# Three gate tiles move from stage 3 of a hybrid RG-LRU and attention layer into its recurrent stage, and work changes engines in the feed-forward stage

## The chip, the cores and the metric

The kernel runs on one core of a Trainium2 chip. The metric is the device time of one execution in microseconds (us); lower is better. The engines are PE (TensorE: matmuls), DVE (VectorE), ACT (ScalarE), POOL (GpSimd) and SP (SyncE, which issues nearly all DMAs). Each of them works through its own queue in order, and semaphores order them against each other.

## The reference: what is computed

Two requests of 512 tokens by 1024 features go through one layer with shared weights. Cut to what matters here:

```python
proj = rmsnorm(x) @ w_in            # 9216 columns, cut into lru_x, lru_gate, q, k, v, gates
xc = dwconv(lru_x)                  # 1280 channels, 4 taps
h = rglru(xc, forward) + rglru(xc, backward)
#   per direction, 16 blocks of 80 channels: r, i = sigmoid(xb @ wa), sigmoid(xb @ wx)
#   a = exp(-8 r softplus(-lam)); u = sqrt(1 - a*a) * i * xc; h[t] = a[t] h[t-1] + u[t]
a_out = (gelu(lru_gate) * h) @ w_lru_out
b_out = dilated_window_attention(q, k, v) @ w_att_out     # 3 groups, merged by their lse
x = x + (sigmoid(g_a) * a_out + sigmoid(g_b) * b_out) @ w_o
gate, val = split(rmsnorm(x) @ w_up)                      # 2 x 3072 columns
x = x + (gelu(dwconv(gate)) * val) @ w_down
```

All is float32.

## The kernel before, in words

**Products.** An fp32 product is made from halves: each operand is cast to a high half (`hi`) and a low half (`lo`, the difference), and three matmuls per 128-row slice sum hi*hi, lo*hi and hi*lo (`mm3`, `prod`). Weights stream through a ring: `Stream` loads raw 128x512 slabs by SP (up to 3 ahead), splits them (`split_to`: the cast to hi on ACT or DVE, the subtraction to lo at line 230 on the engines listed in `lo_eng`, in turn), and holds at most 8 split slabs (`adv`, `take`, `done`). The scheduler keeps the order in which each engine's instructions are written.

**Stage 1 (to 414 us).** `steps1` lists 10 steps "L" (an LRU input tile, convolved by `lru_conv`) and 16 steps "G" (a tile of the attention and LRU gates, through a tanh to DRAM). A step is two halves of 24 matmuls, one for each request. After each half `lru_slot(LRU_RATE)` adds its rate to a credit (capped at 1.5) and, at a credit of 1, issues the next item of recurrent work: `lru_first(n)` (one direction of block n: 8 small matmuls `psg` at lines 456 and 457, tanh and exp on ACT, two DVE products at 467 and 468; then the scan of block n-1) or `lru_second(n)` (the other direction, and the preparation of block n+2). A gate product waits in PSUM until DVE has taken the one before it.

**Stage 2 (to about 974 us).** q, k and v for three groups, with attention between.

**Stage 3 (to about 1096 us).** Ten gate tiles c = 0 to 9 of lru_gate, two halves each, `h_load`, gelu, times h: request 0 stays in SBUF (`held`, `y_split`), request 1 goes to `y_d`. In the first `ATT_DONE` = 3 tiles the attention runs out. Tile c also loads the three attention results of token tile c-2 (`comb_load`, into a ring of six `cg` buffers) and merges them three ticks later (`combine`: DVE, then two adds on POOL at 876 and 877). For token tiles 4 to 7 the merged tile is stored to `o_d` by POOL's queue one tick later. `defer(n, f)` runs f at the n-th next `tick`; there is one tick per half, and the calls due at one tick run in the order in which they were deferred. What is left runs in a loop of ticks at the stage's end.

**Mix and w_o (to about 1352 us).** `th_load` fetches the tanh tiles, into SBUF bytes that the `cg` ring had; `mix_tile` makes 42 matmuls and hands its PSUM tile (two of them) to DVE at 1002 and 1003.

**FFN (to 1865 us).** Each of 24 tiles of w_up is made in a form with 7 products of 12 matmuls in place of 8, which needs sums of weight pieces (`up_split`: S1 = A21 + A22, S2 = S1 - A11, S3 = A11 - A21, S4 = A12 - S2, at line 259, on POOL) and sums of the input (`sums_T`, whose PSUM tile is taken from the pool "t" for the last two token tiles). `batch0(f)` makes the two products A11 and A12; then its PSUM tile `pa` is copied to `p1` by DVE (line 1213; by ACT for f below `EARLY` = 4). `rest(f)` adds the product of S2 into the same `pa`, so that this product waits for the copy; then follow S1, S3, S4 and A22, the convolution on DVE (1246, 1248), the gelu on ACT (1250), and two products on DVE (1252, 1257). After each product `prod` calls `ws.done` and `ws.adv`, and only then does its caller issue the DVE read of the result:

```python
pa, pb = bank(nm), bank("B")
prod(pa, ws.take(1)[0], "B11", True)      # matmuls; then ws.done, ws.adv -> up_split of a later slab
p1[f] = row("p1", 2)
A.copy(out=p1[f], in_=pa) if f < EARLY else V.tensor_copy(out=p1[f], in_=pa)
```

With the ring full, the slab split there is the one eight further on: after A11 of tile f it is A12 of tile f+1, which is the call of `up_split` that makes S1 and S2; S3 and S4 follow the split of S2, one product later.

**Down.** 12 pairs of hidden tiles (`h_pair`: cast on ACT, low halves on the two engines named) times w_down; each PSUM tile `psd`, of eight, is added into the output by DVE at 1330.

Of the kernel before, what the change touches and what calls it, by code (L numbers as in the profile page):

```python
# [20 lines left out]
T = 1024  # L21
# [13 lines left out]
NEG = -1e30  # L35
LRU_RATE = 0.9
O_ORDER = ((0, 0), (0, 1), (1, 0), (1, 1))
# [76 lines left out]
def layer_kernel(ctx: ExitStack, tc: tile.TileContext, xs_in, norm1_g, w_in, conv_w, conv_b, lru_wa, lru_ba,  # L114
# [17 lines left out]
    h_d = dram.tile([RNN, T], F32, name="h_d")  # L132
    y_d = dram.tile([RNN, S], F32, name="y_d")
    sg_d = dram.tile([2 * D, T], F32, name="sg_d")
# [44 lines left out]
    for c in range(3, KR):  # L179
        steps1 += [("G", c - 3), ("L", c)]  # L180
    steps1 += [("G", c) for c in range(KR - 3, 16)]
    specs = []
    for t, c in steps1:
        specs += col_slabs(w_in, C_LRU + 128 * c if t == "L" else C_GA + 128 * c, KD)
    for i in range(9):
        base = (C_V, C_K, C_Q)[i % 3] + 512 * (i // 3)
        specs += [row_slab(w_in, k, base, "ab"[i % 2]) for k in range(KD)]
    for c in range(KR):
        specs += col_slabs(w_in, C_GATE + 128 * c, KD)
# [67 lines left out]
    def up_split(f, nm):  # L257
        w = lambda key: upw[f, key]
        add = lambda out, x, y, op: G.tensor_tensor(out=out, in0=x, in1=y, op=op)
        if nm == ("S2" if f < EARLY else "A12"):  # L260
            upw[f, "S1"] = up_pool[0].tile([128, 512], F32, tag="s1", bufs=1, name="s1")
            upw[f, "S2"] = up_pool[0].tile([128, 512], F32, tag="s2", bufs=1, name="s2")
            add(w("S1"), w("A21"), w("A22"), ALU.add)
            add(w("S2"), w("S1"), w("A11"), ALU.subtract)
        out = split_to("a", w(nm))
        if nm == "S2":
            add(w("A21"), w("A11"), w("A21"), ALU.subtract)
            upw[f, "S3"] = w("A21")
            add(w("A12"), w("A12"), w("S2"), ALU.subtract)
            upw[f, "S4"] = w("A12")  # L270
        if nm == "A22":
            for key in [x for x in upw if x[0] == f]:
                del upw[key]
        return out
# [308 lines left out]
    for s, (typ, c) in enumerate(steps1):  # L583
        if s < 2:
            continue
        slabs = ws.take(2)
        ps = ps1.tile([128, 2, 512], F32, tag="m", bufs=2, name="ps")
        main_mm(ps[:, 0], 0, slabs)
        tick()
        lru_slot(LRU_RATE)  # L590
        main_mm(ps[:, 1], 1, slabs)
        ws.done("a", 2)
        tick()
        ws.adv(2 if s < len(steps1) - 4 else 3)
        if typ == "L":
            lru_conv(c, ps)
        else:
            th = lp.tile([128, 2, S], F32, tag="xc", bufs=2, name="sgt")
            act(out=th, in_=ps, func=AF.Tanh, scale=0.5)
            defer(1, lambda c=c, th=th: SP.dma_start(out=sg_d[128 * c:128 * c + 128],  # L600
                                                     in_=th.rearrange("p b t -> p (b t)")))
        lru_slot(LRU_RATE)
# [301 lines left out]
    ATT_DONE = 3  # L904
    h_load(0)
    for c in range(KR):
        if c == ATT_DONE:
            assert not (units or infl or infl2 or pend)
# [4 lines left out]
            for cc in list(held):  # L913
                y_split(cc, held.pop(cc))
        slabs = ws.take(2)
        for b in range(2):
# [11 lines left out]
            if b == 1:  # L928
                ws.done("a", 2)
                if c + 1 < KR:  # L930
                    h_load(c + 1)
                if c >= 2:
                    cg = comb_load(c - 2)
                    defer(3, lambda t=c - 2, cg=cg: combine(t, cg))
            tick()
            ws.adv(1)
            hT = hts.pop((c, b))
            if b == 0 and c < ATT_DONE:
                gl = p3.tile([128, S], F32, tag="yhold", bufs=ATT_DONE, name="yhold")
# [4 lines left out]
            if b == 1:  # L944
                defer(1, lambda c=c, gl=gl: SP.dma_start(out=y_d[128 * c:128 * c + 128, :], in_=gl))
            elif c < ATT_DONE:
                held[c] = gl
            else:
                y_split(c, gl)
        step[0] += 1  # L950
    lo_eng[:] = [V, G]
    ws.adv(8)
    while later:
# [122 lines left out]
    def hook0(n, i):  # L1076
        if 1 <= n <= KR:
            y_split(n - 1, ystage.pop(n - 1))
        if n < KR:
            ystage[n] = mp.tile([128, S], F32, tag="yst", bufs=3, name="yst")  # L1080
            SP.dma_start(out=ystage[n], in_=y_d[128 * n:128 * n + 128, :])
        if n < 4:
# [199 lines left out]
    banks[1] = batch0(1)  # L1282
    sums(3, pf["t"], "t")
    sums(0)
# [3 lines left out]
    pace[0] = 2  # L1288
    lo_eng[:] = [G]
    sums(1)  # L1290
# [8 lines left out]
    for f in range(NF):  # L1299
# [3 lines left out]
        if f == EARLY:  # L1303
            pace[0] = 2
        pa = banks.get(f) if f < EARLY else batch0(f)
        if f == NF - 1:
            h_pair(0, (V, G))
        rest(f, pa)
    close(cm_f, cm_b, *cm_pf[::-1])


    cm_ps, ps5 = open_pool("ps5", space=PSUM)
    cm_d, dp = open_pool("accd")
    for t in range(8):
        acc[t] = dp.tile([128, D], F32, name=f"accd{t}")
        SP.dma_start(out=acc[t], in_=acc_d[128 * t:128 * t + 128, :])
    for f in range(0, NF, 2):
        w4 = ws.take(4)
        hh, hl = hT.pop(f)
        for t in range(8):  # L1320
            tl = slice(128 * t, 128 * t + 128)
            for hlf in range(2):
                ps = ps5.tile([128, 512], F32, tag="t", bufs=8, name="psd")
                cl = slice(512 * hlf, 512 * hlf + 512)
# [16 lines left out]
        ws.adv(2)  # L1341
    close(cm_d, cm_acc, cm_x20, cm_sa, cm_rp, cm_ps)

# [32 lines left out]
```

## Time and profile before

| | |
|---|---|
| median of 3 runs | 2132.16 us (2132.09 to 2134.18) |
| the profiled execution | 2135.13 us, of which span 2133.4 us |
| mean granted TensorE clock | 0.984 |
| busy: PE, DVE, ACT, POOL | 2032.3, 1259.0, 840.2, 796.0 us |
| moved by DMA | 218.71 MB |

The span runs from the first to the last instruction of the profiled execution; the rest of its time lies around it. Busy times are summed over the span and overlap between engines. A matmul's own duration overlaps the next one's, so the share of PE says little; how many matmuls there are in a stretch says more.

### The profile page before, as it was taken

The page shows a single profiled execution, that of the slowest core. Times are in us where ns is not written, and L with a number is a line of the kernel's source. Part 1 is how long each engine was busy: PE and PEld are TensorE (multiplying, and loading weights), DVE is VectorE, ACT ScalarE, POOL GpSimd, SP SyncE. Part 2 cuts the span into 40 slices and gives each one's busy share as a digit, 9 for nine tenths or more (in the row PEclk, how much of TensorE's full clock was granted, in tenths as well). Part 3 has the DMA queues.
Part 4 walks back from the last instruction along what each step waited for, and adds up shares of the span by engine and source line. Part 5 has one row for each costly group of instructions (what it writes and reads, how often), then busy time and mean ns, then how long its engine had stood idle before and what let it go on. Part 6 is the DMA issues. An engine that isn't in the chain of part 4 may idle for free.

```text
span 2133.4 us, 26437 instructions
## 1 busy us (share of the span) xinstructions
PE 2032.3 (95%) x9571; PEld 1707.6 (80%) x9571; DVE 1259.0 (59%) x1844; ACT 840.2 (39%) x1437; POOL 796.0 (37%) x681
## 2 busy tenths in 40 slices
PE   8989888999999999999999999778899999999999
PEld 6867666787899999998778788657788888788887
DVE  5599998627862671675665565634444444455555
ACT  4488888612431242135433332323333333321210
POOL 3111111034213421413342222487777777632421
PEclk9999999999999999999999999989999999999999
DMA  4535444411111112103556464312222223352322
GB/s 145 155 98 142 122 121 128 157 46 44 31 41 50 35 51 60 30 16 120 193 167 221 160 206 137 105 50 89 89 71 88 81 87 90 124 187 84 107 91 79
DMA packets 203776, 218.71 MB, mean 103 GB/s; under 512 B 28892, under 2 KB 148222, under 8 KB 203646
## 3 DMA queue, kind: packets, MB, share of 16 engines
q1 hardware_dynamic: 201278, 210.73, 31.9%
q0 software_dynamic: 2368, 6.29, 1.1%
q8 instruction: 76, 1.25, 0.3%
q14 instruction: 54, 0.44, 0.1%
HBM read 161.73 MB, written 50.00 MB: 99 GB/s over the span
## 4 chain that ended last, share of the span: by engine, by line
PE 72%; DVE 13%; issue 6%; POOL 4%; ACT 4%; DMA 2%; DVEq 0%; SPq 0%; POOLq 0%; ACTq 0%
PE ps L807 7%; PE ps L808 6%; PE ps L809 6%; PE ps L151 4%; PE ps L153 4%; PE ps L152 4%; PE psd L1328 4%; PE psd L1327 4%; PE psd L1329 4%; PE pfA L1198 3%; PE pfA L1200 3%; PE pfA L1199 3%; DVE u L486 3%; PE o L728 3%; PE pfC L1199 2%
## 5 line engine op out<-in xcount | busy, mean ns | idle before, releaser
L230 POOL TENSOR_TENSOR lo<-raw,hi 128x512 fp32r<-128x512 f32 (+1 forms) x263 | 341.0, 1305 | 640.7 <-ACT hi L227 607.3
L227 ACT CAST hi<-raw 128x512 fp32r<-128x512 f32 (+1 forms) x352 | 204.3, 606 | 302.3 <-PE psd L1329 152.4
L807 PE MATMUL ps<-hi,xh 128*128 128x512 f32 x576 | 251.4, 436 | 0.0
L808 PE MATMUL ps<-lo,xh 128*128 128x512 f32 x576 | 228.4, 397 | 0.0
L809 PE MATMUL ps<-hi,xl 128*128 128x512 f32 x576 | 228.3, 396 | 0.0
L151 PE MATMUL ps<-xh,hi 128*128 128x512 f32 x544 | 216.0, 397 | 0.3 <-DVE xc L403 0.3
L152 PE MATMUL ps<-xl,hi 128*128 128x512 f32 x544 | 214.9, 395 | 0.0
L153 PE MATMUL ps<-xh,lo 128*128 128x512 f32 x544 | 214.1, 394 | 0.0
L1330 DVE TENSOR_TENSOR accd<-accd,psd 128x512 f32<-128x512 f32 x192 | 130.6, 686 | 114.3 <-PE psd L1329 108.9
L807 PEld LDWEIGHTS ps<-hi,xh 128*128 128x128 f32 x576 | 156.1, 271 | 9.6 <-issue 0.2
L808 PEld LDWEIGHTS ps<-lo,xh 128*128 128x128 f32 x576 | 158.3, 275 | 6.0
L809 PEld LDWEIGHTS ps<-hi,xl 128*128 128x128 f32 x576 | 156.3, 271 | 8.0
L1327 PE MATMUL psd<-hi,hp 128*128 128x512 f32 x384 | 150.0, 391 | 3.1 <-DVE gc L1257 3.1
L1329 PE MATMUL psd<-hi,hp 128*128 128x512 f32 x384 | 150.1, 391 | 0.0
L1328 PE MATMUL psd<-lo,hp 128*128 128x512 f32 x384 | 150.1, 391 | 0.0
L707 ACT ACTIVATE p<-p,nm 128x128 f32<-128x128 f32 (+1 forms) x192 | 81.7, 426 | 146.2 <-DVE nm L705 146.1
L1198 PE MATMUL pfA<-T,hi 128*128 128x512 f32 x288 | 116.0, 403 | 23.3 <-DVE p L1213 7.6
L629 DVE TENSOR_REDUCE ss<-sq 128x8 f32<-128x512 f32 x48 | 32.9, 685 | 163.7 <-ACT sq L626 163.7
L151 PEld LDWEIGHTS ps<-xh,hi 128*128 128x128 f32 x544 | 104.2, 192 | 24.5 <-issue 1.4
L153 PEld LDWEIGHTS ps<-xh,lo 128*128 128x128 f32 x544 | 103.8, 191 | 22.2
L152 PEld LDWEIGHTS ps<-xl,hi 128*128 128x128 f32 x544 | 103.9, 191 | 21.8
L1200 PE MATMUL pfA<-T,lo 128*128 128x512 f32 x288 | 114.7, 398 | 1.1 <-POOL lo L230 1.1
(257 smaller groups left out, 4567.3 us busy)
## 6 DMA issues: line engine op xcount, KB each, us to landing
raw<-in_w_in_dram SPq DMA_DIRECT2D x144, 256.0 KB
raw<-in_w_up_dram SPq DMA_DIRECT2D x56, 256.0 KB
r<-in_w_up_dram SPq DMA_DIRECT2D x48, 256.0 KB
f_d<-gc SPq DMA_DIRECT2D x24, 512.0 KB
raw<-in_w_down_dram SPq DMA_DIRECT2D x48, 256.0 KB
hraw<-f_d SPq DMA_DIRECT2D x24, 512.0 KB
sg_d<-sgt SPq DMA_DIRECT2D x16, 512.0 KB
raw<-in_w_lru_out_dram SPq DMA_DIRECT2D x32, 256.0 KB
```

The costliest lines, as they stand in the source:

```text
L151: PE.matmul(out=ps, lhsT=a, rhs=b, start=(k == 0), stop=False)
L152: PE.matmul(out=ps, lhsT=a, rhs=rl(k), start=False, stop=False)
L153: PE.matmul(out=ps, lhsT=wl(k), rhs=b, start=False, stop=(k == n - 1))
L227: A.copy(out=hi[:, 0:n], in_=r[:, 0:n])
L230: e.tensor_tensor(out=lo[:, 0:n], in0=r[:, 0:n], in1=hi[:, 0:n], op=ALU.subtract)
L807: PE.matmul(out=ps, lhsT=a, rhs=hi, start=(k == 0), stop=False)
L808: PE.matmul(out=ps, lhsT=a, rhs=lo, start=False, stop=False)
L809: PE.matmul(out=ps, lhsT=b, rhs=hi, start=False, stop=(k == KD - 1))
L1198: PE.matmul(out=ps, lhsT=a, rhs=bh[:, k], start=(start and k == 0), stop=False, **kw)
L1327: PE.matmul(out=ps, lhsT=hh[:, i, tl], rhs=w[0], start=(i == 0), stop=False)
L1328: PE.matmul(out=ps, lhsT=hh[:, i, tl], rhs=w[1], start=False, stop=False)
L1329: PE.matmul(out=ps, lhsT=hl[:, i, tl], rhs=w[0], start=False, stop=(i == 1))
```

## The change

- `EARLY_Y` = 3: the gate tiles c = 0, 1, 2 become steps "Y" at the end of `steps1`, for both requests at once (gelu, times h loaded from `h_d`, whole rows to `y_d`, which grows to both requests). Stage 3 runs over c = 3 to 9, and loads request 0 of the three early tiles back into the `yhold` buffers. `LRU_RATE` falls from 0.9 to 0.8.
- The merges get a table, `combs`: after tile index i of stage 3 it loads one or two token tiles, and merges them two and three ticks later.
- The four sums of `up_split` go from POOL to DVE. `lo_eng` is [G, V] from before the fourth `batch0` until tile f = 5, and [G] from there (before: [G]). At the end of stage 3 it is [V] for the fill of the ring and [V, G] after it (before: [V, G] for both).
- `sums(3)`, which needs the pool "t", moves behind the third `batch0`. The low halves of the first `h_pair` are both made on POOL.
- The eight PSUM tiles of down come from a pool of six and one of two.

```diff
-LRU_RATE = 0.9
+LRU_RATE = 0.8
+EARLY_Y = 3
-    steps1 += [("G", c) for c in range(KR - 3, 16)]
+    steps1 += [("G", c) for c in range(KR - 3, 16)] + [("Y", c) for c in range(EARLY_Y)]
...
-        add = lambda out, x, y, op: G.tensor_tensor(out=out, in0=x, in1=y, op=op)
+        add = lambda out, x, y, op: V.tensor_tensor(out=out, in0=x, in1=y, op=op)
...
+        elif typ == "Y":
+            gl = lp.tile([128, 2, S], F32, tag="xc", bufs=2, name="gl")
+            ht = lp.tile([128, 2, S], F32, tag="xc", bufs=2, name="ht")
+            SP.dma_start(out=ht.rearrange("p b t -> p (b t)"), in_=h_d[128 * c:128 * c + 128])
+            act(out=gl, in_=ps, func=AF.Gelu_apprx_tanh)
+            V.tensor_tensor(out=gl, in0=ht, in1=gl, op=ALU.mult)
+            defer(1, lambda c=c, gl=gl: SP.dma_start(out=y_d[128 * c:128 * c + 128],
+                                                     in_=gl.rearrange("p b t -> p (b t)")))
...
-    h_load(0)
-    for c in range(KR):
-        if c == ATT_DONE:
+    combs = {2: (0,), 3: (1, 2), 4: (3,), 5: (4, 5), 6: (6, 7)}
+    h_load(EARLY_Y)
+    for c in range(EARLY_Y, KR):
+        i = c - EARLY_Y
+        if i == ATT_DONE:
...
+            for cc in range(EARLY_Y):
+                t = p3.tile([128, S], F32, tag="yhold", bufs=ATT_DONE, name="yback")
+                SP.dma_start(out=t, in_=y_d[128 * cc:128 * cc + 128, 0:S])
+                defer(2, lambda cc=cc, t=t: y_split(cc, t))
...
-                if c >= 2:
-                    cg = comb_load(c - 2)
-                    defer(3, lambda t=c - 2, cg=cg: combine(t, cg))
+                for j, t in enumerate(combs.get(i, ())):
+                    cg = comb_load(t)
+                    defer(2 + j, lambda t=t, cg=cg: combine(t, cg))
...
+    lo_eng[:] = [V]
+    ws.adv(8)
     lo_eng[:] = [V, G]
-    ws.adv(8)
...
-    sums(3, pf["t"], "t")
     sums(0)
     sums(0)
     batch0(2, "C")
     ws.hold = len(specs)
     pace[0] = 2
-    lo_eng[:] = [G]
+    lo_eng[:] = [G, V]
+    sums(3, pf["t"], "t")
...
+        if f == EARLY + 1:
+            lo_eng[:] = [G]
         pa = banks.get(f) if f < EARLY else batch0(f)
         if f == NF - 1:
-            h_pair(0, (V, G))
+            h_pair(0, (G, G))
...
     cm_ps, ps5 = open_pool("ps5", space=PSUM)
+    cm_ps_b, ps5b = open_pool("ps5b", space=PSUM)
+    nd = 0
...
-                ps = ps5.tile([128, 512], F32, tag="t", bufs=8, name="psd")
+                ps = (ps5.tile([128, 512], F32, tag="t", bufs=6, name="psd") if nd % 8 < 6 else
+                      ps5b.tile([128, 512], F32, tag="t", bufs=2, name="psd"))
+                nd += 1
```

## Rows read from the trace of the kernel before

**Rows 1.** The page, part 1: busy us (share of the span) and instructions.

```profile
...
PE 2032.3 (95%) x9571; PEld 1707.6 (80%) x9571; DVE 1259.0 (59%) x1844; ACT 840.2 (39%) x1437; POOL 796.0 (37%) x681
...
```

**Rows 2.** Four stretches: us, busy (count) by engine, clock, DMA share, GB/s.

```profile
...
1352.00:1510.00 158.00, 121.45 (x493) 95.81 (x493) 79.39 (x92) 54.21 (x90) 117.49 (x90) 0.90 0.27 81
1510.00:1853.00 343.00, 343.00 (x1513) 283.59 (x1511) 155.30 (x215) 117.95 (x180) 244.34 (x194) 1.00 0.28 86
974.00:1120.00 146.00, 138.23 (x674) 113.81 (x672) 85.66 (x200) 67.98 (x123) 56.66 (x46) 0.99 0.50 162
81.00:392.00 311.00, 278.19 (x1164) 213.46 (x1163) 283.73 (x280) 261.24 (x258) 35.28 (x42) 0.97 0.44 119
...
```

**Rows 3.** Stage 1: TensorE's longest wait and VectorE's low halves, 100 to 400 us.

```profile
...
PE psg L456 <- DVE u L467: 26.5, 12, 4.4
...
L230 DVE TENSOR_TENSOR lo<-raw,hi 128x512 fp32r<-128x512 f32 x38 | 24.3, 682 | 0.0
...
```

**Rows 4.** Stage 1: the last gate group and the last tanh, timeline.

```profile
...
389.87 0.40 PE L456 MATMUL psg<-x,w 120*80 120x512 f32 x1
...
414.01 1.02 ACT L599 ACTIVATE sgt<-ps 128x1024 f32<-128x1024 f32 x1
...
```

**Rows 5.** Stage 3: one combine, from VectorE's first to GpSimd's last, timeline.

```profile
...
1036.45 0.16 DVE L861 TENSOR_TENSOR cm<-cg 128x8 f32<-128x8 f32 x1
...
1042.13 1.60 POOL L877 TENSOR_TENSOR cg<-cg 128x512 f32<-128x512 f32 x1 [0.68 <-POOL cg L876]
...
1111.17 1.62 POOL L877 TENSOR_TENSOR cg<-cg 128x512 f32<-128x512 f32 x1 [0.69 <-POOL cg L876]
...
```

**Rows 6.** End of stage 3: SP's waits, and TensorE's wait.

```profile
...
SPq L982 <- POOL cg L877: 5.6, 1, 5.6
SPq L853 <- DMA o_d<-cg: 2.6, 2, 2.3
...
1120.83 0.76 PE L151 MATMUL ps<-yh,hi 128*128 128x512 f32 x1 [5.18 <-DVE thb L1003]
...
```

**Rows 7.** FFN start, 1352 to 1510: TensorE's waits (total us, times, longest us).

```profile
...
PE pst L1124 <- ACT T L1143: 11.7, 2, 9.8
PE pfA L1198 <- DVE p L1213: 7.6, 2, 5.6
...
```

**Rows 8.** VectorE and GpSimd on two SBUF inputs each at once, timeline.

```profile
...
1437.51 1.66 DVE L1248 SCALAR_TENSOR_TENSOR gc<-g,vff,gc 128x511 f32<-128x511 f32 x1
...
1439.86 0.75 DVE L1248 SCALAR_TENSOR_TENSOR gc<-g,vff,gc 128x511 f32<-128x511 f32 x1
...
1436.88 1.74 POOL L230 TENSOR_TENSOR lo<-r,hi 128x512 fp32r<-128x512 f32 x1
...
```

**Rows 9.** One steady FFN tile, timeline of VectorE, GpSimd, ScalarE and TensorE.

```profile
...
1617.35 0.68 DVE L1257 TENSOR_TENSOR gc<-gc,pfA 128x512 f32<-128x512 f32 x1
1617.94 0.69 DVE L1213 COPY p<-pfA 128x512 f32<-128x512 f32 x1
...
1617.29 1.30 POOL L230 TENSOR_TENSOR lo<-raw,hi 128x512 fp32r<-128x512 f32 x1 [4.52 <-ACT hi L227]
1618.55 1.29 POOL L259 TENSOR_TENSOR s<-r,r 128x512 f32<-128x512 f32 x1
...
1616.61 1.12 ACT L227 CAST hi<-raw 128x512 fp32r<-128x512 f32 x2
...
1618.96 0.39 PE L1198 MATMUL pfA<-T,hi 128*128 128x512 f32 x1
...
```

**Rows 10.** A wait with no change of pace behind it, TensorE timeline.

```profile
...
1461.30 0.47 PE L1198 MATMUL pfA<-T,hi 128*128 128x512 f32 x1 [3.58 <-DVE u L1230]
...
```

**Rows 11.** End of the FFN and start of down, TensorE and GpSimd timeline.

```profile
...
1855.02 0.47 PE L1198 MATMUL pfA<-T,hi 128*128 128x512 f32 x1 [1.71 <-DVE u L1232]
...
1867.90 0.50 PE L1327 MATMUL psd<-hi,hp 128*128 128x512 f32 x1 [3.08 <-DVE gc L1257]
...
1854.34 2.39 POOL L1275 TENSOR_TENSOR hp<-hraw,hp 128x1024 fp32r<-128x1024 f32 x1 [4.52 <-ACT hp L1274]
...
```

More of the change, by code (lines that the diff above doesn't have):

```diff
@@ L132, in layer_kernel @@
     h_d = dram.tile([RNN, T], F32, name="h_d")
-    y_d = dram.tile([RNN, S], F32, name="y_d")
+    y_d = dram.tile([RNN, T], F32, name="y_d")
     sg_d = dram.tile([2 * D, T], F32, name="sg_d")
@@ L180, in layer_kernel @@
         steps1 += [("G", c - 3), ("L", c)]
-    steps1 += [("G", c) for c in range(KR - 3, 16)]
+    steps1 += [("G", c) for c in range(KR - 3, 16)] + [("Y", c) for c in range(EARLY_Y)]
     specs = []
     for t, c in steps1:
-        specs += col_slabs(w_in, C_LRU + 128 * c if t == "L" else C_GA + 128 * c, KD)
+        specs += col_slabs(w_in, {"L": C_LRU, "G": C_GA, "Y": C_GATE}[t] + 128 * c, KD)
     for i in range(9):
@@ L904, in layer_kernel @@
     ATT_DONE = 3
-    h_load(0)
-    for c in range(KR):
-        if c == ATT_DONE:
+    combs = {2: (0,), 3: (1, 2), 4: (3,), 5: (4, 5), 6: (6, 7)}
+    h_load(EARLY_Y)
+    for c in range(EARLY_Y, KR):
+        i = c - EARLY_Y
+        if i == ATT_DONE:
             assert not (units or infl or infl2 or pend)
@@ L937, in layer_kernel @@
             hT = hts.pop((c, b))
-            if b == 0 and c < ATT_DONE:
+            if b == 0 and i < ATT_DONE:
                 gl = p3.tile([128, S], F32, tag="yhold", bufs=ATT_DONE, name="yhold")
@@ L944, in layer_kernel @@
             if b == 1:
-                defer(1, lambda c=c, gl=gl: SP.dma_start(out=y_d[128 * c:128 * c + 128, :], in_=gl))
-            elif c < ATT_DONE:
+                defer(1, lambda c=c, gl=gl: SP.dma_start(out=y_d[128 * c:128 * c + 128, S:T], in_=gl))
+            elif i < ATT_DONE:
                 held[c] = gl
@@ L1080, in hook0 @@
             ystage[n] = mp.tile([128, S], F32, tag="yst", bufs=3, name="yst")
-            SP.dma_start(out=ystage[n], in_=y_d[128 * n:128 * n + 128, :])
+            SP.dma_start(out=ystage[n], in_=y_d[128 * n:128 * n + 128, S:T])
         if n < 4:
@@ L1341, in layer_kernel @@
         ws.adv(2)
-    close(cm_d, cm_acc, cm_x20, cm_sa, cm_rp, cm_ps)
+    close(cm_d, cm_acc, cm_x20, cm_sa, cm_rp, cm_ps_b, cm_ps)
 _INS = ['x_prompt', 'x_sample', 'norm1_g', 'w_in', 'lru_conv_w', 'lru_conv_b', 'lru_wa', 'lru_ba', 'lru_wx', 'lru_bx',
```

## The prediction

> **What bounds the kernel now.** I read the page's busy shares first: PE 95% [rows 1]. The stretches come second, and there one counts matmuls. In the steady FFN, 1513 matmuls fill 343.00 us: 0.2267 us each at full pace, the unit of all sums below [rows 2]. Stage 1 has 1164 in 311 us. They need 263.9 us, so 47 us are lost, while DVE is busy for 283.7 of the 311: DVE sets that pace, and PE's longest wait there is for DVE's product at line 467 [rows 2, 3]. The start of the FFN has 493 in 158 us, 32 of them short transposes (some 3.5 us); 461 need 104.5 us, so 50 us are lost, POOL is busy for 117.5, and PE waits for results that stand behind POOL's [rows 2, 7]. Stage 3 and the steady FFN are PE's own. The waits come third, and the timeline last, for one question: which DVE instruction has how much time to spare in the steady FFN.
>
> **The three gate tiles, -15 us.** Taken from stage 3: 3 x 48 matmuls, 32.6 us. Given to stage 1: after the last gate group (block 15, second direction) PE had two tiles left, from 389.87 to the tanh at 414.01 [rows 4]. At a rate of 0.8, written out half by half, that group comes two steps later in the list, and three tiles follow it: one tile more behind the LRU, 10.9 us. Before it stand four halves more, which PE can fill into its 47 lost us if DVE's work stays as it is; DVE gets four low halves more at 0.68 [rows 3], 2.7 us, and I allow 1 us for a later start and 3 for the extra halves without an item (eleven against seven), in which DVE may run dry. So stage 1 grows by 17.6 and the kernel shrinks by 15.0. Bounds: with DVE never dry, 10.9, thus -21.7; with all of the moved work on the path, 0. The loads of h and the gelus of the new steps lie behind the last group, where DVE has nothing else; slabs are split ahead, so the SP queue, which now waits for a store before each load of h, has some 8 us in hand.
>
> **The merges, +4 us.** One takes 7.3 us from DVE's first to POOL's last instruction (1036.45 to 1043.73) [rows 5]. The last one ended at 1112.79 [rows 5]; SP held a load of the mix stage until then, 5.6 us, and PE waited 5.18 until 1120.83 [rows 6]. Now the two last merges both stand behind the last tile, so the chain ends one DVE share later, 5.7 us. A buffer of the ring is also needed while a store to `o_d` is still behind the next merge in POOL's queue; SP waited 2.6 us for such stores [rows 6], and I allow the same. Against it: the reset turn of `lo_eng` puts the low half that stood ahead of DVE's reads on POOL, some 4 us of the 8 between 1112.79 and 1120.83. Sum +4; bounds -4 and +25 (two rounds of merge, store and load in series).
>
> **The start of the FFN, -20 us.** The 50 lost us are the terms. What stays or comes: about 2 ahead of the first product; the wait of 9.8 for the "t" pool [rows 7] becomes one of some 6 for the bank that DVE's next sum frees, since `batch0(2)` now fills part of it; 3 at the first `rest`, 4 for the input sums that stay on POOL; then DVE is the fullest engine: per tile seven reads or products at 0.69, four convolution steps at 0.75 [rows 8, 9], four sums and two or three low halves, and 1.2 for the gelu make about 14, with waits 16, against PE's 5 x 12 x 0.2267 = 13.6. That is 2.5 for each of three tiles, 4 for the fourth and the refill of the ring, and 3 for a slow clock after the longer waits. Sum 30, gain 20. Bounds: -8 (DVE's queue holds PE as long as POOL's did in half of the tiles) to -32.
>
> **The sums in the steady FFN, +53 us.** This term decides. Look at one tile [rows 9]: DVE's product at 1257 starts at 1617.35, the copy `p1` at 1617.94, ends at 1618.63, and PE's next product into that bank starts at 1618.96. The copy has 0.33 us to spare. The calls put S1 and S2 of the next tile between these two DVE instructions: `prod` splits A12 of the next tile before its caller issues the copy. On POOL they delayed nobody. On DVE, alone, they take 2 x 0.68 (as the row of 1257), and the copy is late by 1.0. But they are not alone: POOL starts low halves at 1617.29 and, with its own sums gone, the next one right behind, because ACT's two casts end at 1617.73. How the two engines share is in rows 8: a DVE step with two SBUF inputs takes 0.75 by itself and 1.66 while POOL works, and POOL's 1.30 becomes 1.74: they alternate, DVE waiting for POOL's instruction and then needing 0.55. So S1 issues at 1617.94, waits for POOL until 1618.55, ends at 1619.1; POOL's next low half runs to 1620.3; S2 ends at 1620.85; the copy ends at 1621.55. PE starts 2.7 us late, in each tile from f = 5 to 22: 18 x 2.7 = 48.6. Nothing gives it back, since the next convolution hangs on PE's products of this tile. Waits of that length sometimes leave PE slow (stage 1 with its waits of up to 4.4 has a clock of 0.97), sometimes not (3.58 us, next matmul at full pace) [rows 2, 3, 10]; 0.25 us each adds 4. Bounds: 18 x 1.0 = 18 if POOL never interferes; 58 with a slow restart each time; below 18 only if the order in DVE's queue is not as I read it. I take 53, as POOL's two casts are ready in the row itself. S3 and S4 follow the copy, 5 us ahead of the next read that matters, and cost nothing.
>
> The Trainium skill (GPSIMD Engine Reference, Specifications) says that GpSimd shares its SBUF interfaces with VectorE, and that instructions with two SBUF inputs contend; by that rule the term is 48.6, where the bare durations give 18; rows 8 agree with the rule.
>
> **Down, -5 us.** DVE's low half of the first `h_pair` held up a read for which PE waited 1.71; on POOL it takes 2.39 and has 8 us. The first `psd` waited 3.08 for the FFN's last product at 1257 [rows 11]: if it waits because of its bank, six banks that are free earlier remove that. Sum 4.8; bounds 0 and 7 (with the slow restart).
>
> **Sum.** -15 + 4 - 20 + 53 - 5 = +17 us, so the profiled execution would go from 2135.1 to 2152, and the median, 3 us below it, from 2132.2 to 2149.
>
> **The rivals.** (1) DVE keeps its access through both sums, or POOL is seldom there: 18 x 1.0 to 1.2, about 20 in place of 53. Then -16: 2116, faster. For it: POOL is busy for 244 of 343 us with sums and will be for some 160 without [rows 2]; against it: its low half starts 0.65 us ahead of S1 in the row [rows 9]. (2) The sums are off PE's path: the copy isn't late at all. Then -36: 2096. For it: DVE is busy in only 155 of 343 us [rows 2]; against it: the 0.33 us. It decides from the point where the copy ends before PE has finished the product between. The Trainium skill (GPSIMD Engine Reference, Engine selection) has a rule by which this would be the outcome: elementwise work on two inputs belongs on VectorE, GpSimd being about twice as slow; the durations agree (0.68 against 1.29), but that rule looks at durations, and not at the queue in which the sums stand. (3) The stores to `o_d` behind the merges hold SP for both rounds, and the mix stage starts some 20 us later: 2169. For it: SP already waits for such a store; against it: buffers other than the stored one come free earlier.
>
> **How the numbers follow.** My forecast 0.60 (2149; its own range 2130 to 2172), rival 1 0.17, rival 2 0.11, rival 3 0.12. A change of 0.2%, 4.3 us, is about what a measurement of this kernel tells from none. Faster holds rival 2, most of rival 1 and a little of the forecast's low end: 0.30. Within 0.2%: 0.08, from both sides of it. Slower: 0.62. The range reaches from 2106, inside rival 1, to 2172.
>
> **What would show it.** In the steady FFN: S1 and S2 between DVE's 1257 and 1213, at 1.1 and 1.7 us, a wait of PE for `p1` of about 2.7 in each tile, and a tile of 21.7 us in place of 84 x 0.2267 = 19.0; were it still 19.0, I was wrong. Stage 1 should end near 431, with DVE still full; stage 3 should lose three tiles; POOL should idle at the start of the FFN while DVE doesn't; the first `psd` should not wait. The prediction falls if S1 and S2 run elsewhere in the queue, or take 0.68 each.

## The result, and the profile after

The changed kernel takes 2219.32 us (median of 3 runs, 2219.28 to 2220.87) against 2132.16: a ratio of 1.041 (95% interval 1.038 to 1.043), 87 us slower. The forecast was 2149. The sign was right and the size was not.

Parts 1 and 5 of the page of the changed kernel: TensorE's busy time, and the costliest wait of a group of its matmuls (the last columns are the idle time ahead of the group and what ended most of it). Line numbers are those of the changed kernel: 1 higher in the helpers and the LRU stage, 9 in the merges, 16 in mix and the FFN, 22 in down.

```profile
...
PE 2060.2 (93%) x9571; PEld 1725.3 (78%) x9571; DVE 1375.4 (62%) x1959; ACT 841.3 (38%) x1434; POOL 675.1 (30%) x563
...
L1214 PE MATMUL pfA<-T,hi 128*128 128x512 f32 x288 | 124.7, 433 | 57.4 <-ACT hi L228 46.7
...
```

TensorE's share fell from 95% [rows 1] to 93%, its busy time rose by 28 us for the same 9571 instructions: part of the loss is idle time and part is slower matmuls. The group shown, which holds the product that waits for the copy `p1`, now has 57.4 us of idle time ahead of it.

Five stretches of the changed kernel by the view of windows (columns as in [rows 2]): the LRU stage, stage 3, the mix stage, the start of the FFN to its 504th matmul, and the rest of the FFN.

```profile
...
81.00:447.80 366.80, 330.70 (x1403) 257.89 (x1402) 307.50 (x311) 283.57 (x284) 42.30 (x44) 0.96 0.45 126
1004.20:1104.20 100.00, 92.81 (x467) 76.16 (x467) 63.54 (x143) 54.39 (x114) 34.90 (x27) 0.98 0.51 162
1104.20:1372.90 268.70, 249.85 (x1121) 205.15 (x1120) 153.52 (x231) 86.52 (x158) 81.01 (x72) 0.97 0.54 172
1372.90:1539.70 166.80, 132.14 (x521) 104.32 (x522) 109.78 (x138) 55.02 (x90) 63.79 (x46) 0.89 0.25 76
1539.70:1950.20 410.50, 368.19 (x1513) 297.37 (x1512) 240.08 (x285) 121.22 (x182) 176.27 (x127) 0.95 0.24 75
...
```

The last row holds as many matmuls as the steady row of [rows 2], 1513, and those took 343.00 us at clock 1.00. They now take 410.5 at 0.95, with TensorE busy for 368. The stages, all bounded by the same instructions in each trace (first product of the attention stage, its last, first of mix, first of the FFN, its 505th, first and last of down), and the profiled executions' times:

| kernel | time | to attention | attention | stage 3 | mix | FFN to 504 | rest of FFN | down |
|---|---|---|---|---|---|---|---|---|
| before | 2135.1 | 413.5 | 555.8 | 127.1 | 258.9 | 162.8 | 345.1 | 265.9 |
| changed | 2220.9 | 447.8 | 556.5 | 100.0 | 268.7 | 166.7 | 410.6 | 264.7 |
| difference | +85.8 | +34.3 | +0.7 | -27.1 | +9.8 | +3.9 | +65.5 | -1.2 |
| forecast | +17 | +17.6 | 0 | -32.6 | +4 | -20 | +53 | -5 |

So 69 us are to be explained: 24 at the start of the FFN, 17 in the LRU stage, 12 in the steady FFN, 6 in mix, 5 in stage 3, 4 in down.

One steady tile after the change, timeline, the rows that answer to [rows 9]; its last three are the product into the bank of `p1`, one matmul in the middle of what follows, and one behind it.

```profile
...
1566.92 0.68 DVE L1273 TENSOR_TENSOR gc<-gc,pfA 128x512 f32<-128x512 f32 x1
1567.52 1.19 DVE L260 TENSOR_TENSOR s<-r,r 128x512 f32<-128x512 f32 x1
1568.75 1.63 DVE L260 TENSOR_TENSOR s<-s,raw 128x512 f32<-128x512 f32 x1
1570.30 0.68 DVE L1229 COPY p<-pfA 128x512 f32<-128x512 f32 x1
...
1566.87 2.97 POOL L231 TENSOR_TENSOR lo<-raw,hi 128x512 fp32r<-128x512 f32 x2 [4.52 <-ACT hi L228]
...
1570.49 0.62 ACT L228 CAST hi<-s 128x512 fp32r<-128x512 f32 x1 [3.17 <-DVE s L260]
...
1571.13 0.47 PE L1214 MATMUL pfA<-T,hi 128*128 128x512 f32 x1 [2.47 <-ACT hi L228]
...
1573.02 0.63 PE L1214 MATMUL pfA<-T,hi 128*128 128x512 f32 x1
...
1575.54 0.39 PE L1214 MATMUL pfC<-T,hi 128*128 128x512 f32 x1
...
```

Behind the product at L1273 stand the two sums (L260), 1.19 and 1.63 us long, and only then the copy `p1` at 1570.30; before, it started 0.59 after the product's start. It ends at 1570.98 and TensorE starts 0.15 later, after 2.47 idle. One us later come matmuls of 0.63 in place of 0.39, at half pace, and 4.4 us after the wait they are back at 0.39. The row names ScalarE's cast as the releaser. That cast does end at 1571.11; but the ring holds eight slabs and a tile uses seven, so its slab should be one of the next tile's. The name is to be mistrusted, and the experiments say which it is.

Half pace does not follow each wait. Three stretches by the view of windows: two of one tile each, from the end of one such wait to the end of the next, and the slow matmuls of the tile above:

```profile
...
1547.70:1571.10 23.40, 20.93 (x84) 16.82 (x85) 13.61 (x17) 6.62 (x11) 9.66 (x7) 0.93 0.22 67
1617.90:1639.60 21.70, 19.32 (x84) 15.66 (x84) 13.53 (x17) 6.54 (x10) 9.68 (x7) 1.00 0.24 71
1572.10:1575.40 3.30, 3.30 (x9) 2.58 (x8) 1.76 (x2) 0.00 (x0) 0.62 (x1) 0.50 0.00 0
...
```

The tile of 23.40 us has a mean clock of 0.93, the one of 21.70 has 1.00 throughout; the slow matmuls ran at 0.50, the lower of TensorE's two levels. From 1524 to 1916 the trace holds 18 of these waits (2.47 each but for two of 2.54 and 2.75) and 17 tiles between them, 13 of 23.4 and 4 of 21.8.

### The profile page after: what moved, and what is told of

It reads as the page before. It is cut to its first block, busy times and chain, and to the rows that moved or that the text cites. A ratio compares the mean times of both kernels' runs of the same rounds, so it can differ in the third digit from the quotient of the medians.

```text
span 2219.1 us, 26493 instructions
## 1 busy us (share of the span) xinstructions
PE 2060.2 (93%) x9571; PEld 1725.3 (78%) x9571; DVE 1375.4 (62%) x1959; ACT 841.3 (38%) x1434; POOL 675.1 (30%) x563
## 5 line engine op out<-in xcount | busy, mean ns | idle before, releaser
L816 PE MATMUL ps<-hi,xh 128*128 128x512 f32 x576 | 252.2, 438 | 11.6 <-ACT gl L602 11.6
L1352 DVE TENSOR_TENSOR accd<-accd,psd 128x512 f32<-128x512 f32 x192 | 130.3, 686 | 111.6 <-PE psd L1351 105.7
L1214 PE MATMUL pfA<-T,hi 128*128 128x512 f32 x288 | 124.7, 433 | 57.4 <-ACT hi L228 46.7
L816 PEld LDWEIGHTS ps<-hi,xh 128*128 128x128 f32 x576 | 156.5, 272 | 21.8 <-ACT gl L602 12.0
L1216 PE MATMUL pfA<-T,lo 128*128 128x512 f32 x288 | 123.3, 428 | 1.0 <-POOL lo L231 1.0
L1215 PE MATMUL pfA<-T,hi 128*128 128x512 f32 x288 | 122.7, 426 | 0.0
L1214 PEld LDWEIGHTS pfA<-T,hi 128*128 128x128 f32 x288 | 59.9, 208 | 79.3 <-issue 42.0
```

The costliest lines, as they stand in the source:

```text
L816: PE.matmul(out=ps, lhsT=a, rhs=hi, start=(k == 0), stop=False)
L1214: PE.matmul(out=ps, lhsT=a, rhs=bh[:, k], start=(start and k == 0), stop=False, **kw)
```

## The experiments

Each is one kernel, run once beside the kernel before where no interval is given. Single times of the kernel before ranged from 2131 to 2139 in these runs, so small effects are read from the stages of the traces, not from the sums. Runs whose edit leaves a stage alone show how far it moves by itself: the start of the attention stage lies at 446.6 to 448.2, the start of the FFN takes 166.0 to 167.5, mix 266.4 to 270.2.

### The steady FFN: what holds the copy

**The late sums back on GpSimd.**

```
-        add = lambda out, x, y, op: V.tensor_tensor(...)
+        e = V if f < EARLY + 2 else G
+        add = lambda out, x, y, op: e.tensor_tensor(...)
```

> The changed kernel with one thing undone: the four weight sums of the tiles from f = 6 on are made on GpSimd again. Theory (the sums stand in VectorE's queue ahead of the copy p1): no wait of TensorE for p1, a tile of 19.07 us as before in place of 23.4 or 21.8, the 18 steady tiles 65 us shorter, 2154 in all. Rival (the weights' high halves come late, since the trace names ScalarE's cast as the releaser): the casts still follow the sums, which are slower on GpSimd, so the wait of about 2.5 stays and the time is 2200 or more. Second rival (the low halves' turn in the tiles before sets the loss): less than 20 us come back.

Measured: 2150.32; rest of the FFN 343.1, no wait of TensorE in it. 69 us came back, 67.5 of them in this stage.

**The sums stay on VectorE, behind the copy.**

```
     def batch0(f, nm="A", mid=None):
-        prod(pa, ws.take(1)[0], "B11", True)
+        prod(pa, ws.take(1)[0], "B11", True, not late)   # late = f > EARLY
         p1[f] = ...
+        if late:
+            ws.done("a", 1); ws.adv(pace[0])
```

> The changed kernel with the sums left on VectorE, but from f = 5 on the step of the ring that splits the next slabs is called after the copy p1 instead of before it; nothing else differs. Theory (order in VectorE's queue): the copy starts right behind the product as in the kernel before, the wait of 2.47 and the slow clock behind it go, the tile is 19.1 to 19.5 us, and the time is 2150 to 2160. Rival (ScalarE's cast of the sum is what TensorE waits for): the sums come later still, the wait grows by about 0.7 a tile, and the time is 2225 to 2235.

Measured: 2149.30; rest of the FFN 343.3, again no wait. One tile of this kernel, timeline of VectorE, ScalarE and TensorE:

```profile
...
1617.88 0.68 DVE L1277 TENSOR_TENSOR gc<-gc,pfA 128x512 f32<-128x512 f32 x1
1618.48 0.68 DVE L1230 COPY p<-pfA 128x512 f32<-128x512 f32 x1
1619.08 0.68 DVE L260 TENSOR_TENSOR s<-r,r 128x512 f32<-128x512 f32 x1
1619.80 1.66 DVE L260 TENSOR_TENSOR s<-s,raw 128x512 f32<-128x512 f32 x1
...
1621.57 1.26 ACT L228 CAST hi<-s 128x512 fp32r<-128x512 f32 x2 [3.30 <-DVE s L260]
...
1619.46 0.39 PE L1214 MATMUL pfA<-T,hi 128*128 128x512 f32 x1
...
```

The same four sums run on the same engine, the second of them at 1.66 us because GpSimd is there too; they stand one place later and cost nothing. This separates order from load. It also rules out the cast that the trace named: TensorE starts this product at 1619.46, 2.1 us before the cast.

**One sum ahead of the copy, one behind.** (The second sum is put on a list that `batch0` empties behind the copy.)

> The changed kernel with only the first of the two sums ahead of the copy p1 from f = 6 on, the second behind it. It asks what the wait itself costs and what the clock behind it adds. In the changed kernel the two take 1.19 and 1.63 us, TensorE waits 2.47, and in most tiles some ten matmuls behind the wait run at half pace. With the first alone the copy should be late by 1.19 less the 0.33 that it has to spare: a wait of 0.85 a tile. If a short wait leaves the clock alone, the steady tile is 19.9 and the time 2219 less 18 x 3.0, 2163 to 2167. If any wait at this place brings the half clock, 21.2 to 21.5 and 2187 to 2193.

Measured: 2166.64; rest of the FFN 361.4. TensorE's waits from 1500 us on (total us, times, longest):

```profile
...
PE pfA L1219 <- DVE p L1234: 14.8, 18, 1.1
...
```

18 waits of 0.82 on average, as expected from 1.19 less 0.33, and 16 of the 17 tiles between them take 20.1 us (one, with a wait of 1.09, 20.4): 19.05, the wait, and 0.25. So at this place a wait of 0.8 leaves the clock alone, and one of 2.47 mostly does not. The trace now names the copy `p` as releaser.

### The tail of the LRU stage

The end of the stage in the changed kernel, timeline of SP, ScalarE and TensorE:

```profile
...
433.02 0.33 SPq L490 DMA_DIRECT2D h_d<-u  x1
433.39 0.43 SPq L604 DMA_DIRECT2D y_d<-gl  x1
...
437.56 1.28 ACT L602 ACT_TABLE_LOAD   x1 [11.35 <-DMA y_d<-gl]
438.85 1.02 ACT L602 ACTIVATE gl<-ps 128x1024 f32<-128x1024 f32 x1
...
446.68 1.02 ACT L602 ACTIVATE gl<-ps 128x1024 f32<-128x1024 f32 x1 [4.82 <-DMA y_d<-gl]
...
447.76 0.80 PE L816 MATMUL ps<-hi,xh 128*128 128x512 f32 x1 [11.62 <-ACT gl L602]
...
```

TensorE had its last matmul of the third moved tile at 435.75. The second moved step's gelu (its table load in the first ScalarE row) waited 11.35 us for the first one's store of y; that store stands in SP's queue behind the LRU's last store of h, which waits 13.8 us for VectorE. The third gelu ended at 447.7 and the attention stage's first product waited 11.62 for it.

**Other buffers for the gelus:** `tag="xc8", bufs=3` for `gl` in place of `tag="xc", bufs=2`.

> The changed kernel with the gelu tiles of the three moved steps in the ring of three buffers that the block convolution uses, so that a gelu no longer takes the buffer that a store is still reading. Theory (the gelus of the last two moved steps waited 11.35 and 4.8 us for stores of y, and the first product of the attention stage waited 11.6 us for the last gelu): that product starts 10 to 11.6 us earlier, near 437, and the time is 2208. Rival (the LRU's last work and the table loads hold the last gelu anyway, or the attention stage gives it back): less than 4 us, 2216 or more.

Measured: 2216.76; the attention stage starts at 444.2, 3.6 us earlier. The rival held, although the gelus' waits for stores are gone. What stands behind them (timeline of this kernel):

```profile
...
435.17 0.33 SPq L490 DMA_DIRECT2D h_d<-u  x1
...
436.07 2.53 SPq L219 DMA_DIRECT2D raw<-in_w_in_dram  x3
...
440.30 0.62 ACT L228 CAST hi<-raw 128x512 fp32r<-128x512 f32 x1 [10.37 <-DMA raw<-in_w_in_dram]
...
443.13 1.02 ACT L602 ACTIVATE gl<-ps 128x1024 f32<-128x1024 f32 x1
...
444.20 0.79 PE L816 MATMUL ps<-hi,xh 128*128 128x512 f32 x1 [6.45 <-ACT gl L602]
...
```

The LRU's last store sits at 435.17, three slab loads behind it, ScalarE's casts wait 10.37 us for the slabs, and the last gelu waits behind the casts.

**And the LRU's last store from GpSimd's queue:** the same, and `(G if n == NB - 1 else SP).dma_start(out=h_d[...])`.

> The changed kernel with the gelu tiles of the moved steps in the ring of three, as in the run with the gelu buffers, and the LRU's very last store to h_d issued from GpSimd's queue in place of SP's. Theory (behind the buffers stands SP's order: that store waits for the LRU's last product, four slab loads wait behind it, ScalarE's casts wait 10.4 us for them, and the last gelu stands behind the casts): the casts no longer wait, and the first product of the attention stage, at 444.2 with the buffers alone, starts at 437 to 439; the time is 2209 to 2212. Rival (the slabs' own buffers or the LRU's chain hold the casts): less than 2 us against the buffers alone, 2215 or more.

Measured: 2209.34; the attention stage starts at 439.5, TensorE's wait is 3.6. The two edits together start the attention stage 8.3 us earlier, of the 11.6.

**The moved steps ahead of the last three gate tiles.**

> The changed kernel with the three moved steps placed ahead of the last three gate tiles of the list in place of behind them; as many steps, the same work. Theory (at the end of the list each moved step hangs on a load of h behind the last store of the LRU in SP's queue, and the attention stage waits for the last gelu): the wait of 11.6 at the first product of the attention stage goes, that product starts at 434 to 438 in place of 447.8, and the time is 2207 to 2211. Rival (the tail waits for the LRU's last work whatever stands there): less than 4 us gained, 2215 or more; or the extra table loads in the middle slow the LRU and the stage ends later.

Measured: 2224.36; the attention stage starts at 453.7. The rival held: the wait for the gelu is gone, but TensorE waits 12.6 us (up to 9.0 at once) for the LRU's own activations in its last groups, and 4.4 for the last gate tile's tanh ahead of the attention stage.

**Rate 0.9 with the tiles moved.**

> The changed kernel with the rate at which the LRU's work is fed set back from 0.8 to 0.9; the three tiles stay in the LRU stage. Theory (the LRU's last store holds SP's queue ahead of the loads that the moved steps need): the LRU ends two steps earlier, the wait of 11.6 falls under 4 us, but the halves in which TensorE waits for VectorE come back, so the attention stage starts at 440 to 446, and the time is 2212 to 2218. Rival (only the wider spread lets the tiles in): it starts at 450 or later, 2222 or more.

Measured: 2218.77; start at 449.2, between theory and rival, and a wait for the gelu of 1.4. The stage is now 35.7 longer than before, more than the moved tiles' 32.6: at 0.9 nothing is absorbed, and TensorE's waits for VectorE's product are 25.8 again (26.5 in [rows 3]; 20.9 in the changed kernel).

Where the time of the stage goes shows at the LRU's last gate group (before: [rows 4]). It starts at 389.87 before, at 401.45 in the changed kernel and at 391.29 in this one; two, three and five whole tiles follow it. The stretch from 81 us to that group, before and in the changed kernel, by the view of windows:

```profile
...
81.00:389.90 308.90, 276.08 (x1155) 212.03 (x1154) 281.63 (x279) 259.30 (x256) 35.28 (x42) 0.97 0.44 120
...
81.00:401.50 320.50, 296.02 (x1251) 229.82 (x1251) 278.87 (x281) 259.73 (x257) 42.30 (x44) 0.97 0.45 125
...
```

TensorE got 96 matmuls more into it. VectorE had no more work, 278.87 us after 281.63, but idled for 41.6 us in place of 27.3 (30.5 at rate 0.9).

### The start of the FFN

**All sums on GpSimd, the low halves still in turn.**

> The changed kernel with the weight sums of all tiles on GpSimd again, the other edits of the start of the FFN kept (low halves in turn, input sums of the fourth operand later). The steady part should be as with the sums of the late tiles alone undone, 2150 without a change at the start. First theory (the early sums on VectorE relieved GpSimd, but waits in the order of the queues took the gain): without them the stretch from the first product to the 504th matmul, 163.2 us with the late sums undone, grows by 8 or more, 2158. Rival (the early sums' engine makes no difference, since ScalarE's casts behind GpSimd's input sums set that pace): within 4 us of 163, 2147 to 2154.

Measured: 2146.32; the stretch to the 504th matmul takes 160.2, against 163.2 with the early sums on VectorE. The rival held, within its 4 us: the early sums on VectorE, as the change has them, cost some 3 us in place of gaining (162.4 to 163.9 in four runs with them there, 159.8 and 160.2 in two without). The longest wait, 10.1 in the changed kernel, is 12.2 here, so it does not need the sums on VectorE. How it arises in the changed kernel (timeline of GpSimd, ScalarE, VectorE and TensorE):

```profile
...
1420.22 1.26 POOL L1145 TENSOR_TENSOR acc<-acc,B 128x512 f32<-128x512 f32 x1
...
1421.52 0.62 ACT L1166 CAST T<-acc 128x512 fp32r<-128x512 f32 x1 [4.39 <-POOL acc L1145]
...
1422.56 1.13 ACT L228 CAST hi<-s 128x512 fp32r<-128x512 f32 x2
...
1423.21 0.82 DVE L231 TENSOR_TENSOR lo<-s,hi 128x512 fp32r<-128x512 f32 x1 [5.40 <-ACT hi L228]
1423.95 1.75 DVE L260 TENSOR_TENSOR r<-raw,r 128x512 f32<-128x512 f32 x1
1425.62 1.75 DVE L260 TENSOR_TENSOR raw<-raw,s 128x512 f32<-128x512 f32 x1
1427.30 0.68 DVE L1253 COPY p<-pfC 128x512 f32<-128x512 f32 x1
...
1428.12 0.76 PE L1214 MATMUL pfC<-B,hi 128*128 128x512 f32 x1 [10.12 <-DVE p L1253]
...
```

GpSimd's input sum ends at 1421.5; the cast of it on ScalarE follows; behind that in ScalarE's queue are the casts of two weight sums; VectorE's low half has been waiting for one of these for 5.40 us; behind the low half stand two weight sums, 1.75 each, and behind them the copy (`p5` in the kernel, `p` in the trace) that frees TensorE's bank. This is work of four engines in series, with VectorE idle in the middle of it.

**The low halves on GpSimd, the early sums on VectorE:** `lo_eng[:] = [G]` in place of `[G, V]` at the start.

> The changed kernel with the low halves of the first FFN tiles all on GpSimd, as before the change; the early weight sums stay on VectorE. Theory (the wait of 10.1 us for the copy p5 comes from VectorE's share of the low halves: it waits for ScalarE's cast, which stands behind a cast of an input sum that GpSimd makes, and the sums and copies stand behind it in VectorE's queue): that wait falls by half or more and the stretch to the 504th matmul, 166.7 us in the changed kernel, falls to 155 to 160; the time is 2208 to 2213. Rival (GpSimd becomes the holder again, with the low halves behind its input sums): the stretch is 165 to 175, the time 2218 or more.

Measured: 2203.53; the stretch takes 150.5, 16.2 less than in the changed kernel, more than expected. The same wait, total and longest:

```profile
...
PE pfC L1214 <- DVE p L1253: 2.5, 1, 2.5
...
```

### The merges

TensorE's waits in stage 3 and at the start of mix in the changed kernel, then SP's from 1100 to 1140 us:

```profile
...
PE ps L152 <- DVE thb L1019: 15.5, 1, 15.5
PE pt L895 <- POOL cg L886: 6.3, 4, 2.5
...
SPq L862 <- POOL cg L885: 15.3, 3, 6.3
SPq L998 <- DMA o_d<-cg: 9.9, 1, 9.9
...
```

The wait for `thb` was 5.18 before [rows 6] and is 15.5; its load waits for a store to `o_d`, and SP had first waited 15.3 us for merges to free the buffers of the last loads.

**The store right behind its merge,** not one tick later.

> The changed kernel with one thing different: the store to o_d is issued right behind its merge instead of one tick later, behind the next merge. Theory (stores behind merges hold the buffers: SP waits 3.5 us for one store and the first load of thb 9.9 us for another): the load of thb is issued up to 8 us earlier, the wait of 15.5 at the second mix tile falls to 7 to 9, and the time is 2211 to 2213. Rival (the buffers are held by the merges themselves: SP waits 15.3 and 3.8 us for GpSimd's additions): at most 3 us, 2216 or more.

Measured: 2218.50; mix 267.3 in place of 268.7, the wait 13.1. The rival held, and 1.4 us lie within what mix moves by itself.

**One merge behind the last tile:** `combs = {2: (0,), 3: (1, 2), 4: (3, 4), 5: (5, 6), 6: (7,)}`.

> The changed kernel with the merges spread otherwise over the steps of stage 3: one, two, two, two, one in place of one, two, one, two, two, so that one merge in place of two stands behind the last gate tile. Issuing the stores at once gave 1.4 us of the 9.8 that the mix stage lost. Theory (the chain of two merges with their loads in series, each load waiting for a buffer that the merge before frees, is what the load of thb waits for): the wait of 15.5 at the second mix tile falls to 5 to 8, the mix stage from 268.7 to 259 to 262, the time is 2209 to 2213. Rival (the same number of merges must pass through the same six buffers, and the chain only starts earlier and waits in stage 3): the mix stage or stage 3 keeps the loss, 2216 or more.

Measured: 2219.46; mix 263.3, and stage 3 105.7 in place of 100.0. TensorE's waits:

```profile
...
PE ps L152 <- DVE thb L1019: 7.6, 1, 7.6
...
PE ps L152 <- ACT gl L957: 5.3, 1, 5.3
...
```

The rival held: the wait is halved and most of it appears one stage earlier. The last merge's first addition on GpSimd starts at 1129.9, at 1128.8 in the changed kernel. Counted in the traces, eight merges start 10.1 us apart on average after the change (1058.20 to 1128.82) and 11.7 before (1027.12 to 1109.20). As the kernel is written, their first load stands on SP behind the attention's last store of numerators (1047.36; 1012.48 before), and from that store to the end of stage 3 there were 84 us and are now 57. The last merge starts 81.5 us after that store in the changed kernel, 81.3 with the stores at once and 82.0 here (96.7 before, when each tile of stage 3 brought one merge). So neither edit shortened the series; which of its loads, buffers and additions sets the 10 us for one merge was not separated.

### Without the move

**Nothing moved** (rate 0.9, `EARLY_Y = 0`, one merge a step), the rest of the change kept, the copy first.

> The kernel with nothing moved (no early steps, rate 0.9, merges one a step, as before), and all other edits of the change kept, the sums in the order with the copy p1 first. By the stage times of the runs so far, moving the three tiles cost 34.3 us in the LRU stage and about 10 us at the start of the mix stage and took 27 from stage 3: so this kernel should be 17 us faster than the one with the copy first and the tiles moved, 2132, if the move is the cause of all three. If the reset turn of the low halves ahead of the mix stage has a part in it, some 4 to 5 us less: 2136. If the move pays and the loss lies elsewhere: 2149 or more.

Measured: 2125.01, 24.3 below the kernel with the copy first and the tiles moved, 7 more than expected, and 10 below the kernel before beside it. So the move costs time here. Mix takes 253.5, 5.4 less than before (255.7 and 253.7 in the next two kernels); the wait for `thb` there:

```profile
...
PE ps L152 <- DVE thb L1019: 1.8, 1, 1.8
...
```

It was 5.18 [rows 6]. In that stage this kernel differs from the one before by the reset turn of the low halves and the layout of `y_d`; no run separates the two.

**That, with all sums on GpSimd.**

> A version put together from the runs: nothing moved (rate 0.9, merges one a step), all weight sums on GpSimd, and the rest of the change kept: the low halves in turn at the start of the FFN and the later input sums, the reset turn of the low halves ahead of the mix stage, both low halves of the first pair on GpSimd, the other banks of the down stage. By the stages of the runs so far: mix stage 253.5 in place of 258.9, start of the FFN 160.2 in place of 162.8, steady part 343.0 in place of 345.1, down 262 in place of 265.9: 14 us below the kernel before, 2118 to 2123. If the parts are not additive, 2125.

Measured: 2122.18, ratio 0.9940 (0.9926 to 0.9954).

**That, with all sums on VectorE behind the copy and the low halves on GpSimd.**

> The version put together before, with two things different: the weight sums of all tiles on VectorE, with the copy p1 first from f = 4 on, and the low halves at the start of the FFN all on GpSimd as before the change. It asks whether the early sums on VectorE pay once no low half stands in VectorE's queue. Theory (the low halves' turn took back what the sums gave; with it undone in the changed kernel the stretch to the 504th matmul was 150.5): the stretch is 147 to 151 in place of 159.8, the rest as there, and the time is 2110 to 2114. Rival (that gain belonged to the other timing of the kernel with the tiles moved): 156 or more, 2118 to 2123.

Here the copy stands first from f = 4 on. Measured: 2108.27, ratio 0.9877 (0.9861 to 0.9894): 1.2% faster than the kernel before. The FFN's two stretches in it:

```profile
...
1351.10:1497.90 146.80, 127.26 (x521) 100.94 (x521) 96.70 (x121) 54.55 (x90) 86.75 (x63) 0.94 0.29 87
1497.90:1841.40 343.50, 343.50 (x1514) 283.56 (x1513) 212.00 (x285) 121.26 (x182) 177.95 (x127) 1.00 0.29 89
...
```

The start takes 146.8 where the kernel before took 162.8 and the changed one 166.7. VectorE has all the sums, and TensorE does not wait for it in the steady part.

## Why the forecast was right and wrong, by its steps

**The sums in the steady FFN: mechanism right, clock mis-sized.** The order in VectorE's queue, the sharing with GpSimd and the wait were read correctly: 2.47 a tile measured against 2.7, the two sums 2.82 us together against 2.91. The Trainium skill (GPSIMD Engine Reference, Specifications) has VectorE's instructions with two SBUF inputs contend with GpSimd. The changed kernel's sums agree, at 0.67 with GpSimd idle (1570.90) and up to 1.77 beside it (1571.50). What failed is "0.25 us each adds 4" for the clock. In the rest of the FFN the 17 waits sum to 42.3 us, and what follows them costs some 25: 1.9 in each of 13 tiles (23.40 less 19.05 and 2.47), 0.25 in the other four. I had chosen by one row, a wait with no change of pace behind it [rows 10]. Even the upper bound of 58 was too low: it puts a slow restart at some 0.5. The trace before held the other answer too. Behind the wait of 3.08 at the start of down [rows 11], by the view of windows:

```profile
...
1869.10:1872.30 3.20, 3.20 (x9) 2.45 (x8) 0.00 (x0) 0.00 (x0) 2.28 (x1) 0.50 1.05 306
...
```

**The start of the FFN: the step that failed most.** Most of the gain of 20 was there to be had: with the low halves left on GpSimd the stretch is 12.3 shorter than before in the changed kernel, and 16.0 in the last version. I had counted VectorE's share of the low halves by its duration, "two or three low halves" in a total of about 14 us a tile, against what TensorE needs. VectorE was far from full there, busy for 109.78 of 166.80 us. A low half waits for a cast, the cast stood behind a cast of GpSimd's sums, and everything behind it on VectorE waited as well: 16.2 us, shown by undoing that edit alone. (The 32 transposes in that step's count are 24 in the trace, a slip of under 2 us.)

**The three gate tiles: half of it failed.** Forecast was a stage longer by 17.6; without the tail's wait it grew by 22.7 (34.3 less 11.6), so 9.9 of 32.6 us were absorbed in place of 15. The sentence that the loads of h and the gelus "lie behind the last group, where DVE has nothing else" missed the order on SP: the LRU's last store stands ahead of the moved steps' stores and of the slabs. Two edits there removed 8.3 of 11.6. The tile behind the LRU cost its 10.9 as forecast; the step that failed is the time up to the last gate group, which came 11.6 later in place of 6.7. VectorE was to run dry for 3 us in the halves without an item, and its idle time grew by 14.3. The runs at rate 0.9 and with the gates last show that place and rate each move the loss and neither removes it.

**The merges: the place right, the cause and the size not.** +9.8 in mix, within the bounds of -4 and +25, and 5.5 of the 32.6 that stage 3 should have lost, TensorE waiting 6.3 there for merges against 2.5 and at a clock of 0.98 against 1.00. Neither of the two that I priced, the stores and the second merge behind the last tile, accounts for it: with the stores at once, and with one merge behind the last tile, the loss stayed. What is left is the series of eight merges, which begins with the attention's end and had been covered by tiles that the change took away; that is argued from the times above, and no run shortened the series. The reset turn and the layout of `y_d` together are worth 3 to 5 without the move, near my 4, and are lost in that wait.

**Down.** The wait of 3.08 for the bank is gone. A later `psd` now waits 1.9, for VectorE's first addition, which waits for the load of the accumulators; I had not asked what is late next:

```profile
...
PE psd L1349 <- DVE accd L1352: 1.9, 1, 1.9
...
```

With the 1.71 at the last FFN tile gone too (it counts in the stage before), 2.9 of the 4.8 came. In the other runs of the changed down stage it takes some 262. The trace shows why it is 264.7 here: behind the 1.9 the clock is 0.50 from 1964.7 to 1968.0, and in the run with the late sums back on GpSimd (262.4) the same wait is 1.2 with no such stretch behind it.

**The rivals.** Rivals 1 and 2 are excluded by the tile above. Rival 3 has the place and, with 9.8 in mix, half of its 20 us, but not the cause: issuing the stores at once gave 1.4.

## What to carry to other kernels

When work moves to another engine, look up which instruction it will stand ahead of in that engine's queue and who waits for that one; the engine's load did not tell it here (VectorE was busy for 240 of 410 us), and one place later in the program made the same work free. An instruction that waits for a third engine takes everything behind it along, so work with late inputs belongs on an engine on which nothing urgent follows. Work that is taken out of a stage also takes away the cover of whatever ran beside it, so time the longest series there before taking it out.

## What the hardware showed that was not expected

A wait of 2.47 us in an otherwise full stream was followed in 13 of 17 cases by some 3.3 us at the lower of TensorE's two clocks (0.50, 1572.10 to 1575.40), which cost 1.6, in the same place of the same loop, and in 4 by none; a wait of 0.8 cost itself and 0.25 in each tile. So in this loop the price of a wait of this length is the wait plus about 1.5 us on average, and one row without the effect proves nothing.
